# The second layer of a two-layer trunk projects its attention pairs and retention heads in another order

## The chip, the cores and the metric

The kernel runs on one core of a Trainium2 chip. The metric is device time in microseconds (us) of one execution. Each core has a matrix engine (TensorE, "PE" in the profile, with its weight loads as "PEld"), three engines for everything else (VectorE "DVE", ScalarE "ACT", GpSimd "POOL"), and a queue engine (SyncE, "SP") which here issues every DMA. Each engine takes its own instructions strictly in the order in which they were written; between engines, semaphores make an instruction wait for its inputs.

## The reference, cut to what matters

```python
def hybrid_layer(x, c_act, norm_g, w_ada, b_ada, w_in, w_out, pos):
    mod = c_act @ w_ada + b_ada
    shift, scale, gate = jnp.split(mod, 3, axis=-1)
    h = rms_norm(x, norm_g) * (1.0 + scale[:, None, :]) + shift[:, None, :]
    proj = h @ w_in
    rq, rk, rv, rg, sq, sk, sv, sg = jnp.split(proj, split_at, axis=-1)
    y_ret = retention(rotary(rq), rotary(rk), rv)         # 4 heads x 128, chunks of 64
    y_ret = y_ret * silu(rg)
    y_sb = stick_breaking(sq, sk, sv) * silu(sg)          # 8 heads x 64, blocks of 128 queries
    y = jnp.concatenate([y_ret, y_sb], axis=-1) @ w_out
    return x + gate[:, None, :] * y

# two layers, then a final RMSNorm; x is 1 x 1024 x 1024, w_in 1024 x 4096, w_out 1024 x 1024
```

In stick-breaking attention the weight of key s for query t is a sigmoid times the running product of (1 - sigmoid) over all the keys between them, so each row of 1024 keys at most needs a scan from right to left. Retention is a linear recurrence over chunks with a decay of its own per head.

## The kernel before, in words

Every product is made of float16 pieces: each operand is split into a high and a low half (`hh` and `hl` for the normalised input, two slots of a weight tile `w`), and three matmuls of 128x512 stand for one exact one. PE therefore has most of the work.

One layer consists of eight projection groups and an output projection. `stick_project(l, p)` (L680) projects attention pair p, two heads of 64: 192 matmuls `acc<-hh,w` and `acc<-hl,w`. I call such a stretch P0 to P3. `retention_project(l, h)` projects retention head h: 192 matmuls `acc<-w,hh` and `acc<-w,hl` in eight tiles of 128 positions, and starts for each tile a chain (`retain`) through DVE, ACT, POOL and DMA with a few small matmuls (`psc`, `po`). These are R0 to R3. `out_project` (L1072 on) makes 16 tiles of 24 matmuls `acc<-w,y`: first the four tiles of positions 0 to 511 for each half of the columns, then the same for positions 512 to 1023. A tile's last pieces are read from the attention output of pair 3, whose second half is complete only when that pair's eighth block is.

Beside the projections each pair's attention runs, one pair after the other (`attend`, L816), eight blocks of 128 queries each, b = 0 to 7. `head_pair` makes the scores (`z<-k,q`) and their sigmoids; for each head `head_block` then runs, on DVE, a scan (`keep<-keep,own`), a product (`beta<-beta,keep`) and, after a copy on ACT, a subtraction (`keep<-beta,keep`), and SP transposes the result into the tile `ta`. `weigh` multiplies two blocks at a time with the values (`av<-ta,vt`).

Buffers limit it: blocks 4 to 7 take four of six 4 KB buffers ("f4") each. Blocks 5 and 6 of pair 3 are an exception in both layers. They borrow the places of `hh` and `hl`, called `home` there, and wait for the mark `through`, which is set when the last projection of the layer is done:

```python
            if p == 3 and b in (5, 6):

                yield [*need, ("through", l)]
                home = apart(big.tile([P, 4, 1024], F32, tag=("hh", "hl")[b - 5], name="home"))
```

The order of the instructions on every engine is made while the program is built. A class `Flow` keeps one estimated clock per engine and lets the stream of highest rank whose inputs it holds to be ready go on. Attention has a higher rank than the projections, so projections fill what attention leaves. The projections themselves are one stream, in the order that `layers()` (L1221) writes: P0 R0 P1 R1 P2 R2 P3 R3. A second list, `groups` (L657), sets the same order for loading and splitting the weights. All instructions are issued through one helper, so the profile puts them on line 83; they are told apart by their tiles.

Of the kernel before, what the change touches and what calls it, by code (L numbers as in the profile page):

```python
# [13 lines left out]
F32 = mybir.dt.float32  # L14
# [5 lines left out]
P = 128  # L20
# [4 lines left out]
NT = S // P  # L25
# [13 lines left out]
def retention_constants():  # L39
    f = np.float32  # L40
    lg = np.log1p(-(f(2.0) ** (f(-5.0) - np.arange(4, dtype=f)))).astype(f)
    i = np.arange(P, dtype=f)
    m, c = i[:, None], i[None, :]
    same = (i[:, None] // 64) == (i[None, :] // 64)
    later = (c // 64) > (m // 64)
    mask = np.zeros((P, 4, P), f)
    qdec = np.exp((i[:, None] + f(1.0)) * lg[None, :]).astype(np.float64)
    for h in range(4):
        dec = np.exp((np.abs(c - m) - (c + 1)).astype(np.float64) * lg[h])
        mask[:, h] = np.where(same | later, dec * np.exp((m - 127.0) * lg[h]), 0.0) * RS  # L50
    kdec = np.exp((f(127.0) - i)[:, None] * lg[None, :]).astype(f)
    bdec = [float(np.exp(f(P) * lg[h])) for h in range(4)]


    cols = np.concatenate([kdec * f(DS * VS), EPS * P * (VS * RS / qdec) ** 2], 1).astype(f)
    return mask, cols, bdec
# [11 lines left out]


MASK, COLS, BDEC = retention_constants()  # L70


class Engine:
# [212 lines left out]
def trunk(ctx: ExitStack, tc, x, c, norm_g, w_ada, b_ada, w_in, w_out, final_g,  # L286
# [3 lines left out]
    pe, act, dve, pool, sp = (Engine(flow, k, e) for k, e in (  # L290
        ("pe", nc.tensor), ("act", nc.scalar), ("dve", nc.vector), ("pool", nc.gpsimd), ("dma", nc.sync)))
# [3 lines left out]
    wk = Slots(flow, ctx.enter_context(tc.tile_pool(name="wk", bufs=2)), 2)  # L295
# [16 lines left out]
    def bank(name, tag="g", bufs=5):  # L312
        return ps.tile([P, 512], F32, tag=tag, bufs=bufs, name=name)
# [5 lines left out]
    def apart(tile):  # L319

        flow.big.add(tile.tensor.name)
        return tile
# [192 lines left out]
    def adapt(l):  # L515
        yield from gate_rows(l)
        if l + 1 < DEPTH:
            yield from modulation(l + 1)
# [130 lines left out]
    def in_pieces(l, first, off):  # L649
        src = w_in[l].rearrange("(k p) (s q) -> k p s q", p=P, s=8)  # L650
        return lambda k: src[k][:, first:first + 4, off:off + P]

    def out_pieces(l, hf):
        src = w_out[l].rearrange("(k p) f -> k p f", p=P)
        return lambda k: src[k][:, hf * 512:(hf + 1) * 512]

    groups = []  # L657
    for l in range(DEPTH):
        for i in range(4):
            groups.append((("P", l, i), in_pieces(l, 4, i * P)))  # L660
            groups.append((("R", l, i), in_pieces(l, 0, i * P)))
        for hf in range(2):
            groups.append((("O", l, hf), out_pieces(l, hf)))

    def three(acc, ah, al, bh, bl, keys, last=False):

        for k in range(NK):
            yield keys(k), None, "pe"
            pe.matmul(acc, ah(k), bh(k), start=(k == 0), stop=False)
            pe.matmul(acc, ah(k), bl(k), start=False, stop=False)  # L670
            pe.matmul(acc, al(k), bh(k), start=False, stop=(k == NK - 1))
            roomw.n += last
# [11 lines left out]
    def stick_project(l, p):  # L684
# [84 lines left out]
        if p == 0:  # L769
            yield from take(2)  # L770
            accs = [bank("acc", "pj", 2) for i in range(2)] + [bank("acc") for i in range(2)]
            if l == 0:
                first = [(col, 0) for col in range(4)] + [(col, 1) for col in range(3)]
                flow.spawn(MAIN, later())
                yield from begin(0, range(4), accs, (0, 0, 1, 1))
                yield [("begun", 0, 1)]
            else:
                first = [(col, 0) for col in range(4)]
                yield from begin(0, range(4), accs, (0, 0, 1, 1))
            flow.spawn(ATTEND, attend(l, p))  # L780
# [12 lines left out]
    def attend(l, p):  # L793
        yield (), rooma.has()
        rooma.n -= 1
        at = {}
        for b in range(NT):
            need = [(o, l, p, i) for i in range(b // 4 + 1) for o in "qk"]
            home = None
            if p == 3 and b in (5, 6):  # L800

                yield [*need, ("through", l)]
                home = apart(big.tile([P, 4, 1024], F32, tag=("hh", "hl")[b - 5], name="home"))
                flow.grain[home.tensor.name] = 1024
            else:
                yield need, room4.has(2 if b < 4 else 4)
                room4.n -= 2 if b < 4 else 4
            flow.spawn(ATTEND, head_pair(l, p, b, at, home))
            if b == 0:
                flow.spawn(ATTEND, weigh(l, p, at))  # L810
        flow.mark(("taken", l, p))
        rooma.n += 1

    def head_pair(l, p, b, at, home):
        q, k = Q[l, p][0]
        n = (b + 1) * P  # L816
        if b < 4:
            betas, keeps = [], []
            for j in range(2):
                both = f4("both")  # L820
                betas.append(both[:, 0:512])
                keeps.append(both[:, 512:])
        elif home is not None:
            betas, keeps = [home[:, j] for j in range(2)], [home[:, 2 + j] for j in range(2)]
        else:
            betas, keeps = [f4("beta") for j in range(2)], [f4("keep") for j in range(2)]
        for beta in betas:
            pool.memset(beta[:, n - 1:n], 0.0)
        qs = slice(b * P, (b + 1) * P)
        for s0 in range(0, n, 512):  # L830
            w = min(512, n - s0)
            ss = slice(s0, s0 + w)
            yield from take(2)
            z = [bank("z") for j in range(2)]
            for i, (a, c) in enumerate(((0, 0), (1, 0), (0, 1))):
                for j in range(2):
                    head = slice(64 * j, 64 * j + 64)
                    pe.matmul(z[j][:, :w], q[head, a, qs], k[head, c, ss], start=(i == 0), stop=(i == 2))
            for j in range(2):
                yield [z[j]], None, "act"  # L840
                act.activation(keeps[j][:, ss], z[j][:, :w], AF.Sigmoid, scale=-0.125)
                wb = w - 1 if s0 + w == n else w
                act.activation(betas[j][:, s0:s0 + wb], z[j][:, :wb], AF.Sigmoid, scale=0.125)
                roomg.n += 1
                if s0 + w == n:
                    flow.spawn(ATTEND, head_block(l, p, b, j, at, betas[j], keeps[j], home))
        if b == NT - 1:
            roomq.n += 1
# [82 lines left out]
                flow.mark(("ys", l, p, ch))  # L931


    def retention_project(l, h):
        hh, hl = H[l]
        g = ("R", l, h)
        yield [("w", g, 0)]
        w = W[g]
        state = [None, {}]
        mask = wk.tile([P, P], F32, tag="rmask", name="mask")  # L940
        sp.dma_start(out=mask, in_=rmask[:, h])
        for b in range(NT):
            ts = slice(b * P, (b + 1) * P)
            yield (), roomrot.has()
            roomrot.n -= 1
            turn = wk.tile([P, 2, 64], F32, tag="rot", bufs=2, name="turn")
            sp.dma_start(out=turn, in_=rot[:, b])
            acc = bank("acc", "pj", 2)
            yield from three(acc, lambda k: hh[:, k, ts], lambda k: hl[:, k, ts],
                             lambda k: w[k][:, 0], lambda k: w[k][:, 1],  # L950
                             lambda k: [("w", g, k), ("h", l, b // 4, k)], b == NT - 1)
            yield (), roomr.has()
            roomr.n -= 1
            flow.spawn(DRAIN, retain(l, h, b, acc, state, turn, mask), [acc, turn])
# [267 lines left out]
    def layers():  # L1222
        xres = x_v
        for l in range(DEPTH):
            last = l == DEPTH - 1
            yield [("h", l, 0, 0)]
            for i in range(4):
                yield from stick_project(l, i)
                if i == 0:
                    rest = adapt(l)  # L1230
                    flow.spawn(SPARE, rest)
                if i == 1:
                    flow.lift(rest, ADAPT)
                yield from retention_project(l, i)
            flow.mark(("through", l))
            xnew = (x1, x2)[l]
            yield from out_project(l, xres, xnew)
            xres = xnew
# [100 lines left out]
    flow.spawn(NORM, start())  # L1339
    flow.spawn(WARM, awake())  # L1340
    flow.spawn(MAIN, layers())
    flow.run()

# [22 lines left out]
```

## Time and profile before

| what | value |
|---|---|
| median of 3 runs | 1103.54 us (1101.24 to 1107.1) |
| the profiled execution, its own time | 1100.85 us |
| its span, first to last instruction | 1098.9 us |
| mean granted TensorE clock | 0.986 of full speed |
| PE busy | 1050.7 us, 96% |
| DVE busy | 878.2 us, 80% |
| ACT busy | 550.5 us, 50% |
| POOL busy | 245.4 us, 22% |

The second layer's projections begin at about 567 us of the span. Its stretches follow from the first matmul of each kind: R0 615 to 668, P1 to 721, R1 to 772, P2 to 821, R2 to 877, P3 to 926, R3 to 981, and the output projection from there to 1090. PE's busy time counts a matmul that runs at the lower clock at its longer duration. In a timeline row "x78" means 78 instructions merged into one piece, and a bracket gives the idle time before it and what ended that. A "granted clock" of 1.00 is 2.4 GHz and one of 0.50 is 1.2 GHz.

### The profile page before, as it was taken

How to read it: one execution, taken by the hardware profiler on the slowest of the kernel's cores; microseconds unless marked ns; L12 is line 12 of the kernel's file. 1: busy time of each engine (PE TensorE's matmuls, PEld its weight loads, DVE VectorE, ACT ScalarE, POOL GpSimd, SP SyncE). 2: the span in 40 equal slices, each digit the busy share in tenths (PEclk: the TensorE clock that was granted, in tenths of full speed). 3: DMA queues.
4: the chain of work that ended last, by engine and by line, in shares of the span. 5: the costliest groups of instructions: out<-in, count | busy, mean ns of one | idle time of the engine just before them, and what ended most of it. 6: DMA issues, size and time to landing. Idle time of an engine off the chain costs nothing.

```text
span 1098.9 us, 18640 instructions
## 1 busy us (share of the span) xinstructions
PE 1050.7 (96%) x6472; PEld 521.7 (47%) x6472; DVE 878.2 (80%) x1673; ACT 550.5 (50%) x1263; POOL 245.4 (22%) x557
## 2 busy tenths in 40 slices
PE   6989999999999999999999999999999999999786
PEld 5644444444455444444445444445444544444343
DVE  3589999899999878996748698878978797878724
ACT  4647464545554564653445545454554555554202
POOL 2571330232023103300010142023202320330002
PEclk9899999999999999999999999999999999999988
DMA  9917575756876664568470846673664566355844
GB/s 296 251 29 184 115 171 127 168 132 161 183 183 164 117 144 80 131 158 225 135 221 13 186 85 142 138 194 69 137 124 95 113 112 146 77 146 138 217 159 143
DMA packets 343901, 159.61 MB, mean 145 GB/s; under 512 B 228032, under 2 KB 319232, under 8 KB 343808
## 3 DMA queue, kind: packets, MB, share of 16 engines
q1 hardware_dynamic: 343808, 158.44, 61.1%
q8 instruction: 50, 0.82, 0.3%
q14 instruction: 43, 0.35, 0.1%
HBM read 92.32 MB, written 11.53 MB: 95 GB/s over the span
## 4 chain that ended last, share of the span: by engine, by line
PE 63%; DVE 12%; issue 7%; DMA 6%; ACT 5%; POOL 3%; SPq 3%; POOLq 0%; DVEq 0%; ACTq 0%
PE acc L83 51%; PE z L83 3%; PE av L83 3%; SPq L83 3%; DVE keep L83 2%; DVE t L83 2%; DVE w L83 2%; PE psc L83 1%; PE sums L83 1%; PE po L83 1%; DMA rqkT<-t 1%; POOL t L83 1%; DMA ta<-keep 1%; DMA wst<-in_w_in_dram 1%; DVE beta L83 1%
## 5 line engine op out<-in xcount | busy, mean ns | idle before, releaser
L83 PE MATMUL acc<-hh,w 128*128 128x512 f16 x1024 | 323.1, 382 | 0.7 <-DVE q L83 0.6
L83 PE MATMUL acc<-w,hh 128*128 128x512 f16 x1024 | 305.0, 379 | 0.0
L83 PEld LDWEIGHTS <-w 128*128 128x128 f16 x1536 | 146.2, 99 | 179.0 <-issue 20.6
L83 PE MATMUL acc<-hl,w 128*128 128x512 f16 x512 | 195.2, 381 | 0.8 <-DVE hl L83 0.8
L83 PE MATMUL acc<-w,hl 128*128 128x512 f16 x512 | 194.0, 379 | 0.0
L83 POOL TENSOR_TENSOR t<-t,t 128x128 f32<-128x128 f32 (+1 forms) x192 | 126.5, 672 | 244.2 <-DVE t L83 204.5
L83 PE MATMUL acc<-w,y 128*128 128x512 f16 (+1 forms) x792 | 173.3, 377 | 5.8 <-ACT y L83 4.8
L83 PEld LDWEIGHTS <-hh 128*128 128x128 f16 x1024 | 92.5, 98 | 97.4 <-issue 10.0
L83 DVE SCALAR_TENSOR_TENSOR w<-wst,w 128x512 f16<-128x512 f32 x160 | 110.9, 715 | 20.6 <-ACT w L83 19.7
L83 PEld LDWEIGHTS <-y 128*128 128x128 f16 x792 | 76.9, 99 | 95.6 <-issue 6.2
L83 DVE TENSOR_TENSOR_SCAN keep<-keep,own 128x640 f32<-128x640 f32 (+3 forms) x56 | 106.2, 1902 | 11.5 <-ACT keep L83 11.5
L83 ACT ACTIVATE w<-wst 128x512 f16<-128x512 f32 x160 | 96.4, 634 | 23.8 <-DMA wst<-in_w_in_dram 16.8
L83 ACT CAST t<-t 128x256 f16<-128x256 f32 (+1 forms) x128 | 44.0, 351 | 98.2 <-POOL t L83 53.1
L83 PEld LDWEIGHTS <-hl 128*128 128x128 f16 x512 | 50.1, 98 | 60.4
L83 ACT CAST keep<-beta 128x640 f16<-128x640 f32 (+3 forms) x56 | 49.5, 884 | 52.1 <-DVE beta L83 51.9
L83 ACT ACTIVATE keep<-z 128x512 f32<-128x512 f32 (+3 forms) x112 | 59.7, 533 | 17.1 <-PE z L83 15.2
L83 PE MATMUL av<-ta,vt 128*64 128x256 f16 (+1 forms) x960 | 56.1, 268 | 9.6 <-DMA ta<-keep 9.4
L83 DVE TENSOR_TENSOR t<-acc,turn 128x256 f32<-128x256 f32 x128 | 48.1, 417 | 21.4 <-ACT vd L83 20.4
L83 PE MATMUL z<-k,q 64*128 64x512 f16 (+3 forms) x576 | 64.1, 326 | 1.0 <-DVE t L83 0.3
L83 DVE TENSOR_TENSOR keep<-beta,keep 128x640 f16<-128x640 f32 (+3 forms) x56 | 57.5, 1030 | 4.2 <-ACT keep L83 4.2
L83 DVE TENSOR_TENSOR_SCAN both<-both,own 128x128 f32<-128x128 f32 (+3 forms) x64 | 55.1, 870 | 7.2 <-ACT both L83 7.2
L83 ACT ACTIVATE beta<-z 128x512 f32<-128x512 f32 (+4 forms) x112 | 60.2, 538 | 0.0
(122 smaller groups left out, 1326.0 us busy)
## 6 DMA issues: line engine op xcount, KB each, us to landing
wst<-in_w_in_dram SPq DMA_DIRECT2D x128, 256.0 KB, 3.6
wst<-in_w_ada_dram SPq DMA_DIRECT2D x64, 256.0 KB, 3.1
ada<-in_w_ada_dram SPq DMA_DIRECT2D x16, 512.0 KB, 6.8
wst<-in_w_out_dram SPq DMA_DIRECT2D x32, 256.0 KB, 3.4
x<-xh SPq DMA_DIRECT2D x24, 256.0 KB, 2.5
xt<-in_x_dram SPq DMA_DIRECT2D x8, 512.0 KB, 5.7
turn<-in_rot_dram SPq DMA_DIRECT2D x64, 64.0 KB, 2.3
xt<-x SPq DMA_DIRECT2D x8, 512.0 KB, 4.4
```

The source lines that it names most:

```text
L83: real(*args, **kw)
```

## The change

A table `ORDER` now gives the order of the groups for each layer, and both `layers()` and the list of weight loads follow it. The first layer keeps its order. The second has P0 R0 P1 P2 R1 P3 R2 R3. The borrowed places are kept in the first layer only; in the second, blocks 5 and 6 of pair 3 take four f4 buffers like those of any other pair, and don't wait for `through`. `retention_project` gets a range of tiles to do, which is all eight in every entry of this table.

```diff
+ALL = range(NT)
+ORDER = ((("P", 0, ALL), ("R", 0, ALL), ("P", 1, ALL), ("R", 1, ALL), ("P", 2, ALL), ("R", 2, ALL), ("P", 3, ALL), ("R", 3, ALL)),
+         (("P", 0, ALL), ("R", 0, ALL), ("P", 1, ALL), ("P", 2, ALL), ("R", 1, ALL), ("P", 3, ALL), ("R", 2, ALL), ("R", 3, ALL)))
...
     for l in range(DEPTH):
-        for i in range(4):
-            groups.append((("P", l, i), in_pieces(l, 4, i * P)))
-            groups.append((("R", l, i), in_pieces(l, 0, i * P)))
+        for kind, i, bs in ORDER[l]:
+            if 0 in bs:
+                groups.append(((kind, l, i), in_pieces(l, 4 if kind == "P" else 0, i * P)))
...
-            if p == 3 and b in (5, 6):
+            if l in (0,) and p == 3 and b in (5, 6):
...
-            for i in range(4):
+            for kind, i, bs in ORDER[l]:
+                if kind == "R":
+                    yield from retention_project(l, i, bs)
+                    continue
                 yield from stick_project(l, i)
...
-                yield from retention_project(l, i)
```

No instruction is added or taken away on any engine; they stand in another order from the end of P1 of the second layer on. On PE, at the end of P1, the next group's first matmuls followed like this before:

```order
L83 LDWEIGHTS w
L83 MATMUL acc<-hh,w 128x512
L83 LDWEIGHTS hh
L83 MATMUL acc<-w,hh 128x512
L83 LDWEIGHTS hh
L83 MATMUL acc<-w,hh 128x512
```

and now, at the same place, like this:

```order
L90 LDWEIGHTS w
L90 MATMUL acc<-hh,w 128x512
L90 LDWEIGHTS w
L90 MATMUL acc<-hh,w 128x512
L90 LDWEIGHTS w
L90 MATMUL acc<-hl,w 128x512
```

Where R1 (weights loaded from `hh`) began, P2 (weights loaded from `w`) begins. On DVE, in the output projection of the second layer, stand the two heads of pair 3's block 7 (`keep` and `beta`, 1024 wide) among the residuals of the output tiles (`up` and `xh`, one pair of rows for each finished tile). Before:

```order
L83 SCALAR_TENSOR_TENSOR keep<-keep,own 128x1024
L83 SCALAR_TENSOR_TENSOR up<-acc,gate 128x512
L83 TENSOR_TENSOR xh<-xh,up 128x512
L83 SCALAR_TENSOR_TENSOR beta<-beta,keep 128x1023
L83 SCALAR_TENSOR_TENSOR xt<-xt,rs,fg 128x1024
L83 TENSOR_TENSOR keep<-beta,keep 128x8x128
L83 SCALAR_TENSOR_TENSOR up<-acc,gate 128x512
L83 TENSOR_TENSOR xh<-xh,up 128x512
L83 TENSOR_TENSOR keep<-beta,keep 128x8x128
```

Now (the first row is the subtraction of the first head, the `keep` rows after it belong to the second):

```order
L90 TENSOR_TENSOR keep<-beta,keep 128x8x128
L90 SCALAR_TENSOR_TENSOR up<-acc,gate 128x512
L90 TENSOR_TENSOR xh<-xh,up 128x512
L90 SCALAR_TENSOR_TENSOR keep<-keep,own 128x1024
L90 SCALAR_TENSOR_TENSOR beta<-beta,keep 128x1023
L90 SCALAR_TENSOR_TENSOR up<-acc,gate 128x512
L90 TENSOR_TENSOR xh<-xh,up 128x512
L90 TENSOR_TENSOR keep<-beta,keep 128x8x128
```

The last subtraction stood behind the eighth residual `up` of the output projection, and now stands behind the fifth. On SP's queue, the last transposes of that block stood here before, among the loads and stores of output tiles:

```order
L83 DMA out_dram<-xt 128x1024
L83 DMA xt<-x_84 128x1024
L83 DMA_TRANSPOSE ta<-keep 128x8x128 x2
L83 DMA x_84<-xh 128x512
L83 DMA_TRANSPOSE ta<-keep 128x8x128 x2
L83 DMA xt<-x_84 128x1024
L83 DMA out_dram<-xt 128x1024 x3
```

and now:

```order
L90 DMA xh<-x_83 128x512 x2
L90 DMA x_84<-xh 128x512
L90 DMA_TRANSPOSE ta<-keep 128x8x128 x2
L90 DMA x_84<-xh 128x512
L90 DMA xh<-x_83 128x512
L90 DMA x_84<-xh 128x512
L90 DMA_TRANSPOSE ta<-keep 128x8x128 x2
L90 DMA xh<-x_83 128x512
L90 DMA xt<-x_84 128x1024
```

No load of a whole finished tile (`xt<-x_84`) and no output (`out_dram`) stands ahead of these transposes any more. On PE, 213 matmuls of the output projection stood ahead of the last `av` of pair 3 and 147 of 128x512 and 48 of 128x256 behind it; now 165 stand ahead of it, and 195 and 48 behind it.

## Rows read from the trace of the kernel before

**Rows 1.** The page: the span, and PE's busy time with its share.
```profile
span 1098.9 us, 18640 instructions
PE 1050.7 (96%) x6472; PEld 521.7 (47%) x6472; DVE 878.2 (80%) x1673; ACT 550.5 (50%) x1263; POOL 245.4 (22%) x557
```

**Rows 2.** Busy time of the engines by stage: R0, R2, P3, R3, the gap.
```profile
core 0: us, PE busy (x) PEld busy (x) DVE busy (x) ACT busy (x) POOL busy (x), PEclk, DMA share, GB/s
...
615.00:668.00 53.00, 52.56 (x336) 25.14 (x334) 46.59 (x102) 28.52 (x76) 19.36 (x37) 1.00 0.67 143
...
821.00:877.00 56.00, 54.92 (x386) 27.53 (x385) 44.63 (x103) 28.84 (x77) 17.50 (x38) 1.00 0.50 105
877.00:926.00 49.00, 48.58 (x283) 22.16 (x281) 43.05 (x69) 28.34 (x60) 7.20 (x18) 1.00 0.59 118
926.00:981.00 55.00, 53.55 (x370) 26.87 (x369) 43.11 (x104) 26.47 (x72) 16.83 (x36) 1.00 0.48 107
...
1036.60:1056.00 19.40, 9.08 (x61) 5.58 (x62) 6.53 (x7) 3.73 (x7) 2.21 (x6) 0.74 0.88 250
```

**Rows 3.** PE's timeline: pair 1's last `av`, then the output projection's end.
```profile
825.50 2.65 PE L83 MATMUL av<-ta,vt 128*64 128x256 f16 x48
...
1019.54 17.01 PE L83 MATMUL acc<-w,y 128*128 128x512 f16 x78
1041.22 0.30 PE L83 MATMUL av<-ta,vt 128*64 128x256 f16 x1 [4.67 <-DMA ta<-keep]
1044.16 0.37 PE L83 MATMUL av<-ta,vt 128*64 128x256 f16 x2 [2.64 <-DMA ta<-keep]
1045.36 4.02 PE L83 MATMUL av<-ta,vt 128*64 128x128 f16 x45 [0.83 <-DMA ta<-keep]
1050.81 0.61 PE L83 MATMUL acc<-w,y 128*128 128x512 f16 x2 [1.44 <-ACT y L83]
1052.21 38.22 PE L83 MATMUL acc<-w,y 128*128 128x512 f16 x193 [0.79 <-DVE y L83]
```

**Rows 4.** PE alone by stage: busy time, granted clock, DMA share, GB/s.
```profile
1045.30:1049.40 4.10, 4.02 (x45) 0.61 0.94 341
...
1056.00:1060.00 4.00, 4.00 (x21) 1.00 0.18 62
```

**Rows 5.** PE's timeline: scores of pair 3's block 4, then of block 5.
```profile
955.85 0.34 PE L83 MATMUL z<-k,q 64*128 64x128 f16 x6
981.65 1.47 PE L83 MATMUL z<-k,q 64*128 64x512 f16 x12
```

**Rows 6.** Timelines of DVE and SP: pair 3's last subtraction, transposes; landing times.
```profile
1033.43 1.22 DVE L83 TENSOR_TENSOR keep<-beta,keep 128x1024 f16<-128x1024 f32 x1
...
1040.76 2.67 SPq L83 DMA_TRANSPOSE ta<-keep  x2
...
DMA to landing us min/median/max: 3.2/4.4/6.1
```

**Rows 7.** Timelines of PE and DVE: block 7 of pair 2.
```profile
906.97 0.82 PE L83 MATMUL z<-k,q 64*128 64x512 f16 x6
...
916.93 2.35 DVE L83 TENSOR_TENSOR keep<-beta,keep 128x1024 f16<-128x1024 f32 x2
...
931.08 1.18 PE L83 MATMUL av<-ta,vt 128*64 128x128 f16 x20 [0.67 <-DMA ta<-keep]
```

**Rows 8.** DVE's timeline: first scans of pair 2's blocks 5, 6 and 7.
```profile
875.52 1.76 DVE L83 TENSOR_TENSOR_SCAN keep<-keep,own 128x768 f32<-128x768 f32 x1
...
896.02 2.02 DVE L83 TENSOR_TENSOR_SCAN keep<-keep,own 128x896 f32<-128x896 f32 x1
...
908.45 4.47 DVE L83 TENSOR_TENSOR_SCAN keep<-keep,own 128x1024 f32<-128x1024 f32 x2 [2.76 <-ACT keep L83]
```

**Rows 9.** POOL's groups by shape: R0's subtraction first, then R3's.
```profile
L83 POOL TENSOR_TENSOR t<-t,t 128x256 f16<-128x256 f32 x7 | 8.4, 1207 | 3.8 <-ACT t L83 3.8
...
L83 POOL TENSOR_TENSOR t<-t,t 128x256 f16<-128x256 f32 x7 | 6.1, 873 | 2.3 <-ACT t L83 2.3
```

More of the change, by code (lines that the diff above doesn't have):

```diff
@@ L931, in weigh, with retention_project @@
                 flow.mark(("ys", l, p, ch))
-    def retention_project(l, h):
+    kept_state = {}
+    def retention_project(l, h, bs):
         hh, hl = H[l]
@@ L938, in retention_project @@
         w = W[g]
[L939 to L942, printed above, removed]
+        if bs[0] == 0:
+            mask = wk.tile([P, P], F32, tag="rmask", name="mask")
+            sp.dma_start(out=mask, in_=rmask[:, h])
+            kept_state[l, h] = [None, {}], mask
+        state, mask = kept_state[l, h]
+        for b in bs:
             ts = slice(b * P, (b + 1) * P)
```

## The prediction

> **What bounds the kernel now.** I read the page first: PE is busy for 1050.7 of 1098.9 us [rows 1], so whatever the change gains has to come out of PE's 48 idle us or out of matmuls that run at the lower clock. The change touches only the second layer, so next I read the busy time by stage. From R0 to R3 PE loses little: 0.44 us in R0, 1.08 in R2, 0.42 in P3, 1.45 in R3 (stage length minus PE's busy time) [rows 2]. One stage is different: from 1036.6 to 1056.0 PE is busy for 9.08 of 19.4 us, at a mean granted clock of 0.74.
>
> PE's timeline shows what happens there [rows 3]. The output projection runs without a pause until 1019.54 + 17.01 = 1036.55. Then PE has run out: all matmuls that can be made without the second half of pair 3's attention are done. It waits 4.67, 2.64 and 0.83 us for the transposes (`ta`) of block 7, makes its `av`, and waits 1.44 and 0.79 us more until `y` is split. That is 10.37 us. The clock fell after the long wait: it is 0.61 in the stretch of the `av` and 1.00 again only from 1056 [rows 4].
>
> Why is block 7 late? The scores of block 4 end at 956.2 and those of block 5 begin at 981.65 [rows 5], just after R3's last matmul: this is the wait for `through`. Blocks 5, 6 and 7 then follow each other through DVE, and the last subtraction ends at 1033.43 + 1.22 = 1034.65 [rows 6].
>
> **The part that the change removes.** I price the gap at the full clock. The waits are 10.37 us. The 48 `av` took 0.30 + 0.37 + 4.02 = 4.69 us; 48 of them took 2.65 at 825.50, so 2.0 us are the clock. The two matmuls at 1050.81 took 0.61; one at full clock is 17.01/78 = 0.218, so 0.2 us. The last piece holds 145 matmuls of 128x512 and 48 of half that width: 145 x 0.218 + 48 x 0.109 = 36.8, against 38.22, so 1.4 us. Together **14.0 us** [rows 3].
>
> The change attacks this twice. Without the wait for `through` block 5 need not stand still for 25 us; and with P3 ahead of R2, pair 3's queries exist long before pair 2 is through, so pair 3's attention can begin inside R2. In PE's order the last `av` now has 165 matmuls of the output projection ahead of it instead of 213, and so 48 x 0.218 = 10.5 us more work behind it. The first 48 of these don't read pair 3's second half, so the split of `y` behind the `av`, some 3 us here (1049.4 to 1052.2), is covered by 10.5 us of matmuls. If all goes by the order, the 14.0 us vanish.
>
> **What may be lost at the same place.** PE takes its queue in order, so if `ta` is late, PE stands at the `av` although other matmuls are ready behind it. Is 165 matmuls late enough? From block 7's last scores to the `av` there are 141 matmuls, 141 x 0.218 = 30.7 us. Pair 2's block 7 needed from 906.97 to 931.08, 24.1 us, within P3 and R3 and with DVE at 43.05 of 49 us in the first of them [rows 2], so 6.6 us are spare [rows 7]. The tighter bound comes from DVE's order: the last subtraction stands behind the residual of the fifth output tile, so it can't start before 120 matmuls are done, and 45 x 0.218 = 9.8 us are left to the `av`. Into these must go the residual (two instructions, about 1.3 us), the subtraction (1.2), and the transposes. The second of two transposes is issued about 1.3 us after the first (half of 2.67) and lands 4.4 us later (3.2 to 6.1) [rows 6]: 1.3 + 1.2 + 1.3 + 4.4 = 8.2 us, a fit, with the longest landing 9.9. But measured from end to end, pair 2 took 931.08 - 919.28 = 11.8 us from the last subtraction to the `av`, with four weight loads on SP between its transposes [rows 7], and pair 3 took 10.7 (1034.65 to 1045.36), with loads of finished tiles around it. By these, 1.3 + 1.2 + 11.8 = 14.3, which is 4.5 us too long. SP's order now has no large load directly ahead of these transposes, so I take a point nearer to the fit: **1.5 us** lost, between 0 and 4.5.
>
> **The stretches that are reordered.** Each matmul, scan and transpose is still there, so the question is whether PE stays fed. I compare each new stretch with the one in the trace that holds the same company. R3 will run beside pair 3's blocks 4 to 6; R0, by the same order, ran beside pair 0's blocks 4 to 6, with DVE at 46.59 of 53 us, and PE lost 0.44 us. R1 and R2 will run beside the end of one pair and blocks 0 to 3 of the next, as R3 did: DVE 43.11 of 55, PE lost 1.45. P2 and P3 will run beside blocks 4 to 6 with no retention; P3 had blocks 6 and 7 and lost 0.42 [rows 2]. R1 moves as a whole behind P2, and R2 behind P3, with their DMAs on SP (`turn`, `rqkT`, `y`, a mask) and their additions on POOL; what they are moved past on SP is the other group's value transposes and the same number of weight loads, and R0 carried this mix too. So the small waits should stay about as they are. I charge **1 us**, between -3 (the small waits of R2, P3 and R3 vanish with the order) and +5 (each of R1, P2, P3, R2 and R3 loses about 1 us more).
>
> One thing has no direct precedent: the pace in P2 and P3. From block 4's scores to block 7's there are 153 matmuls in P2 and 138 in P3 with 60 `av` and 36 `z`: 33.4 and 30.1 us plus about 7 for the small ones, so 40.6 and 37.4 us for three blocks. In P3 one block's step, 6 to 7, took 908.45 - 896.02 = 12.4 us; three such make 37.2, and blocks 4 and 5 are shorter. The step from 5 to 6, begun at R2's end, took 20.5 us [rows 8]. I take the first, since it lies wholly within a P stretch.
>
> POOL shows that the company matters: the retention's subtraction of 128x256 averages 1207 ns in R0, with large scans beside it, and 873 ns in R3, where the scans were small [rows 9]. With R3 like R0, seven of them cost 7 x 0.334 = 2.3 us more on POOL, all off PE's path unless they delay block 7. This is inside the 4.5 us allowed above.
>
> The Trainium skill has a rule that speaks against the change here: "SBUF — State Buffer", section "SBUF: two separate sides", says that GpSimd and a VectorE instruction with two SBUF inputs take a shared port pair in turn, whole instruction by whole instruction, the other blocked. The trace agrees, with the 1207 against 873 ns. By it R3's chains get slower with the large scans now in R3, and if all of the 2.3 us reached the last `av` the sum would be 1094 in place of 1092.
>
> **The sum.** -14.0 + 1.5 + 1.0 = -11.5 us. The profiled execution took 1100.85 us (span 1098.9 and 1.95 around it); it would take 1089.3. The median of the runs is 2.7 us above that execution, and I predict that median's successor: 1103.54 - 11.5 = **1092 us**. What remains at the end, from the last matmul at 1090.4 to 1098.9, is untouched.
>
> **Rivals.**
> *Block 7 is still late.* The gap shrinks and moves to the new `av`. Price: a stall of 4.5 us, and since a wait of 4.67 was followed by the lower clock here, the same 3.6 us of slow matmuls: -14.0 + 4.5 + 3.6 + 1 = -4.9, so 1098.6. For it speaks the end-to-end time of 10.7 to 11.8 us; against it the queue without loads.
> *The attention can't keep its pace in P2 and P3 (slower than before).* Mechanism: in an unmixed P stretch block after block has to pass one chain with six f4 buffers of which each takes four, and PE, in order, waits at the `av` of pairs 1 and 2. At the mean of the two measured steps, 16.45 us, three blocks need 49.4 us, which is 8.8 and 12.0 us more than the order gives: -14.0 + 20.8 = +6.8, so 1110. It turns to a loss when the two lags exceed 14 us, at a mean step of about 15.3 us. Against it: the 12.4 us step was for a larger block than 4 or 5 and within P3, beside the same projection.
> *The gain is spread away.* Each reordered stretch costs some 2 us more, the five together 10: 1103.5 - 14 + 1.5 + 10 = 1101, no change. For it: DVE is at 78 to 88% in the R stretches, so there is little to catch up with; against it: R0, at 88%, lost 0.44 us.
> *More than planned.* The `av` doesn't wait and the small waits go too: -14.0 - 3 = -17, so 1086.5.
> That the change doesn't do what it says I leave out: the order shows P2 directly behind P1 and no `through` in front of block 5.
>
> **Chances.** Forecast, 1088 to 1096: 0.60. Block 7 late, 1096 to 1101: 0.19. Spread away, 1098 to 1105: 0.08. Slower, by the pace of P2 and P3: 0.08. More than planned: 0.05. What a measurement of this kernel can tell from no change is about 0.5%, 5.5 us, so faster means below 1098.0. That holds the forecast, the larger gain and about half of the late block: 0.74; within 0.5%: 0.18; slower: 0.08. The range runs from 1086.5, the larger gain, to 1101, the end of the late block; above it lie the slower case and part of the spread, about 0.12.
>
> **What would show it.** In the stages of the changed kernel: PE busy for all but a few us of the output projection, the clock at 1.00 through it, no wait over 5 us for `ta`; the waits of PE within P2 to R3 at 4 to 7 us in all. Right in kind and wrong in size would be a wait at the last `av` of 3 us or more with a clock below 1 behind it. The forecast is wrong if PE's waits for `ta` in P2, P3 or R1 come to over 5 us: then the pace was the limit, and not the wait for `through`.

## The result, and the profile after

The changed kernel takes 1091.84 us (median of 4 runs, 1085.35 to 1093.62), the kernel before 1105.32 (median of 4, 1101.24 to 1109.87). The ratio is 0.9864, with a 95% interval of 0.9825 to 0.9902: about 13.5 us faster, where 11.5 were forecast. That the forecast of 1092 us is met to 0.2 us is luck: the median before, from one more run, lies 1.8 us above the 1103.54 that I started from, and the gain is 2.0 us above the forecast.

The gap of [rows 3] is gone. PE's timeline at the same place, the end of the output projection's first part, the last `av` and the rest:

```profile
1006.75 24.77 PE L90 MATMUL acc<-w,y 128*128 128x512 f16 x114
1031.44 2.65 PE L90 MATMUL av<-ta,vt 128*64 128x256 f16 x48
1034.03 47.50 PE L90 MATMUL acc<-w,y 128*128 128x512 f16 x243
```

No bracket stands behind any of the three, so nothing waited. The 48 `av` take the 2.65 us that they take at the full clock, and all 243 remaining matmuls run in one piece. All waits of PE from 560 us on come to three groups (what waited, for what: us in total, times, longest):

```profile
PE psc L90 <- DMA rqkT<-t: 2.5, 2, 1.3
PE psc L90 <- POOL t L90: 0.9, 4, 0.3
PE acc L90 <- DVE q L90: 0.6, 1, 0.6
```

That is 4.0 us; none of it is for `ta`. The stages of the second layer, P2, R1, P3, R2, R3, and the output projection up to the last `av`, answer to [rows 2]:

```profile
core 0: us, PE busy (x) PEld busy (x) DVE busy (x) ACT busy (x) POOL busy (x), PEclk, DMA share, GB/s
...
725.00:776.80 51.80, 51.80 (x285) 22.39 (x283) 38.33 (x46) 26.82 (x54) 0.79 (x8) 1.00 0.59 139
776.80:831.60 54.80, 54.25 (x376) 27.12 (x375) 50.09 (x112) 30.34 (x81) 19.03 (x39) 1.00 0.51 115
831.60:884.70 53.10, 53.10 (x340) 24.32 (x339) 42.51 (x65) 30.59 (x66) 5.60 (x18) 1.00 0.59 115
884.70:938.50 53.80, 52.38 (x352) 25.90 (x351) 48.94 (x113) 30.09 (x80) 19.69 (x40) 1.00 0.53 112
938.50:992.50 54.00, 53.74 (x370) 27.28 (x368) 51.11 (x118) 29.53 (x81) 23.62 (x44) 1.00 0.52 115
992.50:1031.40 38.90, 38.90 (x205) 17.76 (x203) 30.18 (x52) 13.51 (x27) 4.00 (x12) 1.00 0.80 201
```

PE is never idle in P2 and P3, and the clock is at 1.00 throughout.

Spans of single executions don't show the size of the change well. The profiled execution of the changed kernel has a span of 1090.0 us, only 8.9 below that of before, although from P0's first matmul to the last matmul of all the second layer takes 1081.5 - 573.5 = 508.1 us, against 1090.4 - 567.1 = 523.3 before. So the second layer gained **15.2 us**, and the part ahead of it, where the two programs are the same, took 6.3 us longer in this execution (last section). I use the length of the second layer for single profiles below and call it L2.

### The profile page after: what moved, and what is told of

It reads as the page before. It is cut to its first block, busy times and chain, and to the rows that moved or that the text cites. A ratio compares the mean times of both kernels' runs of the same rounds, so it can differ in the third digit from the quotient of the medians.

```text
span 1090.0 us, 18647 instructions
## 1 busy us (share of the span) xinstructions
PE 1053.6 (97%) x6472; PEld 525.4 (48%) x6472; DVE 879.2 (81%) x1673; ACT 550.7 (51%) x1263; POOL 247.7 (23%) x557
## 5 line engine op out<-in xcount | busy, mean ns | idle before, releaser
L90 POOL TENSOR_TENSOR t<-t,t 128x128 f32<-128x128 f32 (+1 forms) x192 | 130.9, 696 | 232.6 <-DVE t L90 196.4
L90 PE MATMUL acc<-w,y 128*128 128x512 f16 (+1 forms) x792 | 170.8, 374 | 3.3 <-ACT y L90 3.1
L90 DVE TENSOR_TENSOR_SCAN keep<-keep,own 128x640 f32<-128x640 f32 (+3 forms) x60 | 114.3, 1911 | 18.8 <-ACT keep L90 18.7
L90 ACT ACTIVATE w<-wst 128x512 f16<-128x512 f32 x160 | 96.5, 635 | 15.2 <-DMA wst<-in_w_in_dram 11.9
L90 ACT CAST keep<-beta 128x640 f16<-128x640 f32 (+3 forms) x60 | 53.0, 885 | 63.5 <-DVE beta L90 63.2
L90 ACT ACTIVATE keep<-z 128x512 f32<-128x512 f32 (+3 forms) x120 | 63.7, 531 | 20.6 <-PE z L90 20.1
L90 DVE TENSOR_TENSOR keep<-beta,keep 128x640 f16<-128x640 f32 (+3 forms) x60 | 61.2, 1024 | 7.5 <-ACT keep L90 7.5
L90 ACT ACTIVATE beta<-z 128x512 f32<-128x512 f32 (+4 forms) x120 | 64.3, 536 | 0.0
L90 DVE SCALAR_TENSOR_TENSOR beta<-beta,keep 128x639 f32<-128x639 f32 (+3 forms) x60 | 62.5, 1047 | 0.0
```

What stands on the lines that cost most here:

```text
L90: real(*args, **kw)
```

## The experiments

The diffs below are against the changed kernel, and "..." stands for lines left out. The theory after the result: PE no longer runs dry because pair 3's attention is done earlier, measured in PE's work. Two things could have done that, the order of the projections and the end of the wait for `through`, and I had argued as if each helped by itself.

**The order alone.**

```diff
-            if l in (0,) and p == 3 and b in (5, 6):
+            if p == 3 and b in (5, 6):
```

> The new order alone; blocks 5 and 6 of pair 3 borrow hh and hl again in the second layer and wait for the mark through. If both parts are needed: block 5's scores stand 3 matmuls into the output projection as they did before, the last av again has 213 matmuls ahead of it, the three waits for ta of about 8 us and the slower clock come back, and the second layer (first matmul of P0 to the last matmul) takes about 521 us against 523.3 before and 508.1 after; time within 0.5% of before. Rival, the order alone brings the gain: no wait for ta over 1 us at the end, about 508 us, 1.2% faster than before.

Measured: 1101.76 us (median of 10), ratio 0.9977 (0.9947 to 1.0007), L2 520.5 us. PE's timeline at the end:

```profile
1016.01 19.60 PE L90 MATMUL acc<-w,y 128*128 128x512 f16 x90
1035.54 0.30 PE L90 MATMUL av<-ta,vt 128*64 128x256 f16 x1
1042.19 0.37 PE L90 MATMUL av<-ta,vt 128*64 128x256 f16 x2 [6.35 <-DMA ta<-keep]
1043.11 3.71 PE L90 MATMUL av<-ta,vt 128*64 128x128 f16 x45 [0.54 <-DMA ta<-keep]
1048.25 0.60 PE L90 MATMUL acc<-w,y 128*128 128x512 f16 x2 [1.44 <-ACT y L90]
1050.12 36.71 PE L90 MATMUL acc<-w,y 128*128 128x512 f16 x193 [1.26 <-DVE y L90]
```

The gap of before is back, row for row. Pair 3's first five blocks are early, but the sixth waits for the end of R3, and what was gained is spent there.

**No borrowed buffers alone.**

```diff
-         (("P", 0, ALL), ("R", 0, ALL), ("P", 1, ALL), ("P", 2, ALL), ("R", 1, ALL), ("P", 3, ALL), ("R", 2, ALL), ("R", 3, ALL)))
+         (("P", 0, ALL), ("R", 0, ALL), ("P", 1, ALL), ("R", 1, ALL), ("P", 2, ALL), ("R", 2, ALL), ("P", 3, ALL), ("R", 3, ALL)))
```

> The old order; blocks 5 and 6 of pair 3 in the second layer take f4 buffers and don't wait for through. If both parts are needed: block 5 starts within R3, but block 7's scores come only after 123 matmuls of the output projection, the last av has 213 ahead of it, so 90 x 0.218 = 19.6 us for a chain that took 24 us in pair 2 and 33 us were given in the new kernel; waits for ta of 5 to 10 us and a lower clock behind them; second layer 517 to 523 us, time 0 to 0.5% below before. Rival, the wait for through was the whole cause, as my prediction put first: block 7 is done by the time PE runs out of matmuls, no wait over 1 us, second layer about 508 us, 1.2% faster than before.

Measured: 1105.09 us (median of 10), ratio 0.9979 (0.9949 to 1.001), L2 523.4 us.

```profile
1015.47 0.82 PE L90 MATMUL z<-k,q 64*128 64x512 f16 x6
1016.23 19.60 PE L90 MATMUL acc<-w,y 128*128 128x512 f16 x90
1036.75 0.27 PE L90 MATMUL av<-ta,vt 128*64 128x256 f16 x1 [0.92 <-DMA ta<-keep]
1042.87 0.37 PE L90 MATMUL av<-ta,vt 128*64 128x256 f16 x2 [5.86 <-DMA ta<-keep]
```

Without the wait for `through` the end is no better at all. Block 7's scores come at 1015.47, and PE has 19.6 us of other work left. So the wait for `through` was not the cause by itself, though the trace of before shows block 5 standing still for 25 us [rows 5]. In the old order blocks 5 to 7, with four f4 buffers each and so one after the other, beside R3 and the output projection, are hardly earlier than the borrowed ones were: the last subtraction ends at 1031.1 us, where it ended at 1034.65, and the last piece of the `av` begins at 1043.8, where it began at 1045.36. **Each half of the change is worth nothing measurable, both together 13.5 us.**

**R2 and P3 change places.** Only the table differs from the changed kernel:

```diff
-... ("P", 2, ALL), ("R", 1, ALL), ("P", 3, ALL), ("R", 2, ALL), ("R", 3, ALL)))
+... ("P", 2, ALL), ("R", 1, ALL), ("R", 2, ALL), ("P", 3, ALL), ("R", 3, ALL)))
```

> As the new kernel, no borrowed buffers in the second layer, but R2 and P3 change places: P0 R0 P1 P2 R1 R2 P3 R3. If the gain comes from blocks 4 to 7 of a pair running beside a projection without retention: pair 1 keeps its fast passage in P2, pair 2's blocks 4 to 6 fall into R2 and take over 60 us instead of 37 to 40, pair 3 starts late, the last av has 213 matmuls ahead of it and the scores of block 7 stand 135 matmuls into the output projection; waits for ta of 5 to 10 us at the end, second layer 518 to 524 us, time within 0.5% of before. Rival, it is enough that block 5 doesn't wait and that P2 comes early: second layer about 508 us, 1.2% faster than before.

Measured: 1101.95 us (median of 10), ratio 0.9952 (0.9918 to 0.9985), L2 517.1 us, a little under what I expected. PE waits 6.55 and 0.54 us for `ta` and 2.8 us for `y` at the end. Pair 1 keeps its passage beside P2, with its first scans of blocks 4 and 7 42.7 us apart (740.92 and 783.66); pair 2's lie at 843.93 and 907.64, 63.7 us apart. This order gains some 6 of the 15 us. It matters therefore that two pairs, not one, pass beside a P stretch.

**Is it retention's company?** This is the passage of a pair's large blocks as DVE's timeline shows it, first scan of block 4 and first scan of block 7. Pair 1 beside R1 in the kernel before, 59.3 us apart:

```profile
744.18 1.48 DVE L83 TENSOR_TENSOR_SCAN keep<-keep,own 128x640 f32<-128x640 f32 x1
...
803.44 4.47 DVE L83 TENSOR_TENSOR_SCAN keep<-keep,own 128x1024 f32<-128x1024 f32 x2 [1.46 <-ACT keep L83]
```

Pair 1 beside P2 and pair 2 beside P3 in the changed kernel, 42.8 and 37.5 us:

```profile
744.97 1.49 DVE L90 TENSOR_TENSOR_SCAN keep<-keep,own 128x640 f32<-128x640 f32 x1 [2.24 <-ACT keep L90]
...
787.72 2.54 DVE L90 TENSOR_TENSOR_SCAN keep<-keep,own 128x1024 f32<-128x1024 f32 x1
...
846.00 1.49 DVE L90 TENSOR_TENSOR_SCAN keep<-keep,own 128x640 f32<-128x640 f32 x1 [0.41 <-ACT keep L90]
...
883.51 2.29 DVE L90 TENSOR_TENSOR_SCAN keep<-keep,own 128x1024 f32<-128x1024 f32 x1 [2.42 <-ACT keep L90]
```

In these stretches DVE is busy for 50.15 of 59.26 us (744.18 to 803.44) and for 32.83 of 42.75 (744.97 to 787.72). That is 17.3 us more work on DVE beside R1, in a passage that is 16.5 us longer; retention's own rows (`t`, `yt`, `rbs` and others) add up to some 22 us there, and to 1.4 beside P2.

To test the cause, the old order without borrowed buffers, as in the second experiment, and with the retention chains of two heads left out:

```diff
...
+            if l == 1 and h in (1, 2):
+                flow.spawn(DRAIN, left_out(l, h, b), [acc, turn])
+                continue
             flow.spawn(DRAIN, retain(l, h, b, acc, state, turn, mask), [acc, turn])
...
```

> The old order P0 R0 P1 R1 P2 R2 P3 R3 without borrowed buffers in the second layer (as e2), with the retention chains of heads 1 and 2 left out there (their projections are still made; the output projection reads head 0's result in their place, so the output is wrong by this). It asks whether it is retention's company that slows blocks 4 to 7 of a pair. If so: beside R1 the first scans of pair 1's blocks 4 and 7 lie about 38 us apart, as in P2 of the new kernel (42.8), and not 59 as before; pair 3 starts early enough and PE doesn't wait for ta at the end, though the order is the old one. 180 small matmuls of about 0.056 us are missing, 10 us, so the second layer takes about 508 - 10 = 498 us. Rival, what counts is the place of P and R themselves: the passage in R1 stays over 50 us, waits of 5 to 10 us at the end come back, about 523 - 10 = 513 us.

Measured: L2 495.4 us, one execution of 1080.95 us. By the estimate above, some 10 us of the difference from before are small matmuls that this kernel doesn't make. Beside R1, whose projection is still made, the same two scans:

```profile
745.70 1.49 DVE L90 TENSOR_TENSOR_SCAN keep<-keep,own 128x640 f32<-128x640 f32 x1 [2.44 <-ACT keep L90]
...
781.22 2.29 DVE L90 TENSOR_TENSOR_SCAN keep<-keep,own 128x1024 f32<-128x1024 f32 x1 [1.11 <-ACT keep L90]
```

35.5 us apart, where they are 59.1 apart in the second experiment's kernel (745.50 and 804.62), and PE has no wait for `ta` from 575 us on, in the order of before. It is the retention chain beside the large blocks that slows their passage, not the projection or the place. (The order of the instructions was made anew for this kernel too; what the run shows is the order and the chip together.)

**What the gap hung on.** Two kernels take away what PE waits for and leave every order as it was before: the old table and the borrowed buffers are back (not shown). First only the `av`:

```diff
...
                     weights = at[i, j][:, sb * 2 + a]
+                    if (l, p, i) == (1, 3, 3):
+                        weights = vt[0][:, 0, 0:2]
```

> The kernel before, except that the last av of pair 3 in the second layer multiplies the values with pieces of themselves instead of ta, so that it needn't wait for block 7; all other instructions and their order are those of before, and the output of the last 256 positions is wrong by this. It prices the gap. If the gap is what my sum says: the waits for ta (8.1 us) vanish, the clock stays up, of the 14.0 us only the waits for y (2.2 us) remain, so about 11.5 us faster than before, second layer about 511.5 us. Rival, the matmuls behind the gap wait for something else just as long (output tiles, buffers): under 4 us faster.

Measured: 1108.42 us (median of 10), ratio 1.000 (0.997 to 1.003), L2 523.6 us. My expectation fell. The `av` no longer waits, but the next output tile does:

```profile
1046.38 1.15 PE L90 MATMUL av<-vt,vt 128*64 128x256 f16 x18
1058.16 1.03 PE L90 MATMUL acc<-w,y 128*128 128x512 f16 x2 [10.63 <-ACT y L90]
```

That `y` is late by another queue: its first half is copied on ACT at 1057.51, right behind the sum of squares of a finished tile (`junk<-xt`, 1056.45), which had waited 6.61 us for that tile's load. So I took that read away as well:

```diff
...
+    far = lambda k, t: t - 4 if (layer[0], k, t // 4) == (1, 7, 1) else t
...
-                yield from three(acc, lambda k: y[:, k, t, 0], lambda k: y[:, k, t, 1],
+                yield from three(acc, lambda k: y[:, k, far(k, t), 0], lambda k: y[:, k, far(k, t), 1],
...
```

> As e3_no_read, and in the second layer the output tiles of positions 512 to 1023 read pair 3's first half in place of its second, so that PE waits neither for block 7's transposes nor for the split of y; the output of those positions is wrong by this. Everything else and every order is that of before. In e3 the wait moved to y, whose first instruction on DVE stands behind two finished tiles (xt) that wait for loads queued on SP behind the transposes. If the gap is two waits in parallel chains and my 14.0 us is its price: no wait left at 1036 to 1060, clock at 1.00, second layer 523.3 - 14.0 = 509.3 us, 1.2% faster than before. Rival, the gap moves on once more (to residuals, buffers or finished tiles): above 515 us.

Measured: 1103.35 us (median of 10), ratio 0.9976 (0.9951 to 1.0001), L2 517.9 us: 5.4 us of the 14.0. The rival was right; the wait moved once more, now to an accumulator that DVE had not emptied.

```profile
1044.96 6.00 PE L90 MATMUL acc<-w,y 128*128 128x512 f16 x27
1058.54 32.77 PE L90 MATMUL acc<-w,y 128*128 128x512 f16 x168 [7.58 <-DVE up L90]
```

DVE's timeline of this kernel, with the finished tiles `xt` in front of `y` and `up`:

```profile
1048.05 1.28 DVE L90 SCALAR_TENSOR_TENSOR xt<-xt,rs,fg 128x1024 f32<-128x1024 f32 x1 [2.61 <-POOL rs L90]
1049.25 0.68 DVE L90 SCALAR_TENSOR_TENSOR y<-av,y 128x512 f32<-128x512 f32 x1
1056.01 1.28 DVE L90 SCALAR_TENSOR_TENSOR xt<-xt,rs,fg 128x1024 f32<-128x1024 f32 x1 [6.07 <-POOL rs L90]
1057.21 0.68 DVE L90 TENSOR_TENSOR y<-y,y 128x512 f16<-128x512 f32 x1
1057.81 0.68 DVE L90 SCALAR_TENSOR_TENSOR up<-acc,gate 128x512 f32<-128x512 f32 x1
```

and its SP queue, where that tile's load was issued behind the transposes:

```profile
1040.93 4.83 SPq L90 DMA_TRANSPOSE ta<-keep  x2
1045.80 0.59 SPq L90 DMA_DIRECT2D x<-xh  x1
1046.43 2.67 SPq L90 DMA_TRANSPOSE ta<-keep  x2
1049.22 0.51 SPq L90 DMA_DIRECT2D xt<-x  x1
```

The old order held the gap open in more than one place: the load of a finished tile stood behind block 7's transposes on SP, that tile's sum of squares stood in front of the first half of `y` on ACT, its scaling stood in front of the second half of `y` and of the residual on DVE, and the residual held the accumulators that PE needed. In the changed order `y` is begun on DVE at 1034.14 and the first finished tile is scaled at 1036.28, and neither waits for a load. This gap went with an order in which everything comes earlier, and not by taking away the one wait that the profile names.

**How near the edge is the new order?** The last subtraction of block 7 made three and seven times:

```diff
         dve.tensor_sub(flat[:, :, 1], whole, flat[:, :, 0])
+        if (l, p, b, j) == (1, 3, 7, 1):
+            for _ in range(2):                       # 6 in the second kernel
+                nc.vector.tensor_sub(flat[:, :, 1], whole, flat[:, :, 0])
```

> The new kernel with the last subtraction of pair 3's block 7 (head 1, second layer) made three times instead of once, on DVE; the output is the same. The transposes start 2 x 1.15 = 2.3 us later. The last transpose was issued at 1025.7 and landings take 3.1 to 5.8 us (median 3.5), the av came at 1031.44 without a wait, so the slack is between 0 and 2.6 us. If it is near 2 us: wait for ta under 1 us, second layer within 1 us of 508.1. Rival, the landing was only just in time: a wait of 2 us or more.

Measured: 1089.99 us (median of 4), ratio 0.9852 (0.9792 to 0.9912), L2 508.8 us, and no wait for `ta`. So at least 2.5 us were spare.

> The same subtraction seven times: the transposes start 6.9 us later. If the slack is about 2 us: PE waits 4 to 5 us for ta, although 48 other matmuls stand ready behind, and if a wait of that size brings the lower clock as it did before, 2 to 4 us more of slow matmuls: second layer 514 to 517 us, 0.6 to 0.8% slower than the new kernel. This is what my rival of a late block 7 priced at 4.5 + 3.6. Rival, PE's queue or the order absorbs it: second layer under 511 us.

Measured: 1099.83 us (median of 10), ratio 0.9928 (0.9896 to 0.9961), L2 515.8 us, 7.7 above the changed kernel.

```profile
1025.42 0.30 PE L90 MATMUL av<-ta,vt 128*64 128x256 f16 x1
1029.22 0.37 PE L90 MATMUL av<-ta,vt 128*64 128x256 f16 x2 [3.50 <-DMA ta<-keep]
1030.44 4.75 PE L90 MATMUL av<-ta,vt 128*64 128x128 f16 x45 [0.84 <-DMA ta<-keep]
1035.12 47.50 PE L90 MATMUL acc<-w,y 128*128 128x512 f16 x243
```

The six extra subtractions took 7.5 us on DVE, and PE waited 3.50 + 0.84 = 4.34 us, so some 3.2 us were spare. The 48 `av` took 5.4 us in place of 2.65, at the lower clock (granted 0.50 from 1030 to 1035). So the wait of 4.3 us cost 7.1; the rest of the 7.7 are small waits of PE elsewhere, 4.7 us in place of 4.0.

**The same in both layers.**

```diff
-ORDER = ((("P", 0, ALL), ("R", 0, ALL), ("P", 1, ALL), ("R", 1, ALL), ("P", 2, ALL), ("R", 2, ALL), ("P", 3, ALL), ("R", 3, ALL)),
+ORDER = ((("P", 0, ALL), ("R", 0, ALL), ("P", 1, ALL), ("P", 2, ALL), ("R", 1, ALL), ("P", 3, ALL), ("R", 2, ALL), ("R", 3, ALL)),
...
-            if l in (0,) and p == 3 and b in (5, 6):
+            if False:
```

> The new order and no borrowed buffers in both layers. In the first layer the trace of before shows at the same place waits of 0.6 us for ta and 3.3 us for y only, so if such gaps are all that the change can remove, the first layer gains 2 to 4 us: 1088 us, 1.5% faster than before, 0.2 to 0.4% faster than the change alone. Rival, the first layer's loads of the second layer's modulation and the next layer's normalisation collide with the moved attention: no gain or up to 5 us lost against the change alone, 1092 to 1097.

Measured: 1097.31 us (median of 6), ratio 0.994 (0.990 to 0.998), against 0.9864 for the changed kernel, so some 5 us are lost again. The second layer keeps its gain (L2 508.2 us), and between 500 and 580 us PE waits for nothing any more, but in the first layer a new gap opens:

```profile
300.00:330.00 30.00, 18.93 (x126) 10.89 (x126) 27.02 (x59) 14.34 (x35) 8.48 (x17) 0.72 0.61 157
```

PE is busy for 18.93 of 30 us (first number after the length), with 10.9 us of waits for R1's last tiles, and DVE for 27.02 (third number). What sets that order there was not taken apart further.

## Why the prediction was right, point by point

- **The gap's price.** 14.0 us were worked out from [rows 3]. L2 fell by 15.2 us, and PE's waits outside the gap went from 5.4 us (15.8 in all from 560 us on, less the 10.4 of the gap) to 4.0, which accounts for the rest. The price and its parts hold: 10.4 us of waiting and 3.6 us of slow matmuls. The seven subtractions show the second part again, as 4.34 us of waiting cost 7.1.
- **The new `av`.** I charged 1.5 us and measured none, with about 3 us spare. The working from DVE's order was near: 45 matmuls behind the fifth residual, then residual, subtraction and transposes. DVE's timeline of the changed kernel has the subtraction, SP's the transposes:

```profile
1023.17 1.22 DVE L90 TENSOR_TENSOR keep<-beta,keep 128x1024 f16<-128x1024 f32 x1
```

```profile
1024.42 2.61 SPq L90 DMA_TRANSPOSE ta<-keep  x2
```

  From the subtraction's end to the `av` at 1031.44 there were 7.0 us (7.3 worked out). Where the `av` does wait, in the kernel with seven subtractions, it starts its last piece 4.5 us after the last of them (1025.92 to 1030.44). The 10.7 and 11.8 us of [rows 6, 7], which I kept as the bad end, held other traffic in SP's queue and don't apply: in [rows 6] SP issued the other head's transposes first, from 1035.04 to 1040.08. In the changed kernel those were issued from 1015.31 to 1018.18, before the last subtraction began.
- **The small waits.** I charged 1 us, between -3 and +5, and the runs give -1.4. These two terms, 1.5 and 1.0 in place of 0 and -1.4, were the mis-sized ones: with them the sum was -11.5, and L2 shows -15.2. The medians' 13.5 lies between.
- **The reason why pair 3 comes early was wrong.** I wrote that with P3 ahead of R2 "pair 3's queries exist long before pair 2 is through", and so its attention can begin inside R2. But in the trace of before pair 3 began (911.07) as soon as pair 2's last scores were made (906.97), and DVE had split its first queries and keys by 891.9: the queries were not what it waited for. What moved it is the passage of pairs 1 and 2 beside P2 and P3, 42.8 and 37.5 us where it was 59.3 and 53.0 (855.48 to 908.45). I had that number and used it only as a risk, in the rival on the pace, and not as the source of the gain. Pair 3's first scores now stand 104.4 us ahead of the output projection (888.07 to 992.51) and stood 69.5 ahead of it before (911.07 to 980.58).
- **"The change attacks this twice"** was wrong in the same way. The two are one: without the early passage block 5 has nothing to gain from not waiting, and with the wait the early passage is lost.
- **The company of the R stretches.** I took R1 and R2 to be like R3 before, DVE at 43.11 of 55 us. Measured were 50.09 of 54.8 and 48.94 of 53.8, and 51.11 of 54 in R3, above R0's 46.59 of 53 [rows 2]. The comparison by blocks left out block 7: its scans now stand in R1 (787.72 and 797.42) and partly in R2 (892.89), while R3 before began after pair 2's (908.45). R3 itself, with blocks 4 to 6, is fuller than R0 was. It did no harm: PE lost 0.55, 1.42 and 0.26 us there. That DVE at 91 to 95% would still feed PE was not something I had shown.
- **Rivals.** The pace in P2 and P3 never became a limit: PE was not idle there, and the scans lie 42.8 and 37.5 us apart, against the 40.6 and 37.4 worked out for the scores from PE's order. The late block was priced at 4.5 + 3.6 us; with seven subtractions it cost 4.3 + 2.8.
- **POOL.** With large scans in R3, its subtraction of 128x256 became slower, as the rows of R0 said: 1160 ns in R3 now, 873 before [rows 9].

```profile
L90 POOL TENSOR_TENSOR t<-t,t 128x256 f16<-128x256 f32 x8 | 9.3, 1160 | 1.5 <-ACT t L90 1.5
```

  The Trainium skill's rule on the shared port pair ("SBUF — State Buffer", "SBUF: two separate sides") is that, of a GpSimd instruction and a VectorE instruction with two SBUF inputs, the one that starts first holds the pair to its end and the other is blocked. Single rows agree: one that met no scan took 0.67 us (at 815.00), and one that began just inside a scan of 896 took 2.32 (at 982.36). But the company of a stage says less than I took it to: in R1 and R2, from which the scans of blocks 4 and 5 moved away, the mean rose as well, from 930 to 1094 ns and from 856 to 1189; in each, one of these subtractions met a scan of block 7 and took over 2 us. None of this made PE wait in R3.

## What to carry to other kernels

When one serial chain and the matrix engine together fill a stage, it can pay to place the chain's long steps beside the work that leaves its engine free, and to put the work that shares this engine (here retention on DVE) beside the chain's short steps. The first layer lost time by the same order, so each place has to be tried. A wait that the profile shows is not yet a cause: take it away alone, and look whether the time follows; here the wait for `through` and the wait for `ta` were both plain to see, and removing either gave nothing. And a wait of PE that lasts some microseconds costs more than its length, because matmuls behind it run at the lower clock: here 4.3 us cost 7.1, the 7.6 us wait for `up` 9.0 (its last piece took 32.77 us, and 31.4 at the full clock), and 10.4 us 14.0.

## What I had not expected of the hardware

Executions of the same instructions reach the second layer up to 9 us apart. P0 of that layer started at 566 to 570 us in six of the profiles whose first layer is unchanged and at 573 to 575 in four. The granted clock from 40 to 60 us was 0.91 in five of the six and 0.78 in the sixth, and 0.68 to 0.72 in the four. The two kernels of this case fall on different sides. The same stretch before and after (PE busy, clock):

```profile
40.00:60.00 20.00, 19.26 (x106) 0.91 0.70 187
```

```profile
40.00:60.00 20.00, 20.00 (x98) 0.69 0.66 170
```

With 0.91 PE even idles a little; with 0.69 it has work all the time and takes it more slowly. What decides it at the start was not tested. For a change of 1% it means that a span of one execution is not enough, and that a length measured from a fixed instruction, as L2 here, says more.
